# Gate one-hots of a hybrid attention, retention and expert layer: eight tokens at a time in bf16

## The chip, the cores and the metric

The kernel runs on one core of one Trainium2 chip. The metric is device time in microseconds (us), the time from the start to the end of one execution on the chip; lower is better. Five engines work side by side: TensorE (PE in the rows; PEld is its loading of weights), VectorE (DVE), ScalarE (ACT), GpSimd (POOL) and SyncE (SP), which here issues the plain DMAs. Each engine takes its instructions in the order of its own queue and waits at the head of it.

## The reference

The layer takes 1024 tokens of width 1024 in front of which 16 learned tokens are put. It adds to them the gated sum of a latent attention and a retention branch, then drops the 16 tokens and adds an expert mixer. Only the mixer matters here. Each token picks, for each of 8 heads, 16 of 128 x 128 experts, so 128 experts in all, each with a gate, and sums them:

```python
s1 = jnp.einsum('thd,kd->thk', q[..., :half], keys_1); s2 = ...   # 128 scores each
v1, i1 = lax.top_k(s1, 16); v2, i2 = lax.top_k(s2, 16)
sc, ci = lax.top_k((v1[..., :, None] + v2[..., None, :]).reshape(T, 8, 256), 16)
# e1, e2: the two key numbers (0 to 127) of each pick
eidx = e1 * 128 + e2; gates = softmax(sc)
act = gelu(einsum('td,tkd->tk', xt, peer_u[eidx]))
y = einsum('tk,tkd->td', gates * act, peer_v[eidx])
```

Inputs and outputs are float32.

## The kernel before

The 8 blocks of 128 tokens are treated in two ways. Three blocks fetch the rows of their experts by indirect DMAs that GpSimd issues (`gathered`: 256 rows of 128x1024 per block, each multiplied or accumulated on VectorE; tiles `row`, `acc`). The other five blocks, 640 tokens, are computed densely in `dense`, over all 16384 experts, and that is where the change lies.

`dense` has two halves. The first runs over `AHEAD` = 48 expert groups, called pieces here: piece `e` holds the 128 experts whose second key is `e`. For each piece, `scores(e)` loads 512 KB (`raw`), splits it into two parts that TensorE multiplies exactly (`whi` on ScalarE, line 218; `wlo` on VectorE, line 219), multiplies them with two segments of the five blocks' activations (`xT`, 384 columns wide, and `x`, 256 wide; lines 246 to 248, into tiles `tr`), applies Gelu (`gl`, line 1159) and stores the result (`gl_d`). The second half runs over groups of eight pieces: it takes `gl` from memory or computes it, multiplies it with the gates (`gt`, line 1210), and multiplies the result (`c_hi`, `c_lo`) with `peer_vt` into accumulators. It needs the gates of all 640 tokens as a dense matrix of first key by second key by token, which lies in memory as `gate_d`.

That matrix is made in `gate_matrix`, in the first half of `dense`, as background work. For each token there are two one-hot matrices of 128 picks by 128 keys: `oa` (line 1119) says which first key each pick has, `ob` (line 1120) which second key, times the pick's gate. One matmul per token (line 1105) with the picks as the contracted dimension gives that token's 128x128 gates. `kt` holds the key numbers and `gT` the gates of a block, with picks on partitions and tokens along the free dimension. Eight tokens make a step, called a batch here: 16 VectorE instructions, 8 matmuls of the batch before, one ScalarE copy out of PSUM (`stage`, line 1106); after four batches `stage` is stored to `gate_d`. There are 80 batches.

The order of background work is set by credit. After each `split_piece`, `pace` adds 6.5 (`pacing["piece"]`, 1.3 times 5 blocks) times the rate to two queues; the gates' queue has rate 0.8, the gathered rows' queue 0.45 (`RATES[4]`). A generator in a queue is advanced while its credit is above zero, and each advance takes off what it yields: 2.0 for a batch, 1.2 for a gathered row. So one piece brings 5.2 / 2.0 = 2.6 batches and 2.9 / 1.2 = 2.4 rows. After piece 47 `finish(0)` runs whatever batches are left, one after the other, and brings no rows meanwhile. Within that program order a scheduler still moves instructions of one engine's queue a little.

Of the kernel before, what the change touches and what calls it, by code (L numbers as in the profile page):

```python
# [12 lines left out]
F32 = mybir.dt.float32  # L13
BF16 = mybir.dt.bfloat16
# [3 lines left out]
AF = mybir.ActivationFunctionType  # L18
OP = mybir.AluOpType
# [4 lines left out]
P = 128  # L24
# [119 lines left out]
def hybrid_layer(ctx: ExitStack, tc: tile.TileContext, out, a, dbg=None):  # L144
    nc = tc.nc
    V, S, T, G = nc.vector, nc.scalar, nc.tensor, nc.gpsimd
    dbg = dbg or {}

    const = ctx.enter_context(tc.tile_pool(name="const", bufs=1))
# [36 lines left out]
    def load_const(name, ap, shape):  # L186
        t = const.tile(shape, F32, name=name)
        nc.sync.dma_start(t, ap)
        return t

    def bcast(ap, n, off=0):
        return bass.AP(tensor=ap.tensor, offset=ap.offset + off, ap=[[0, P], [1, n]])
# [86 lines left out]
    def zacc(name="zacc"):  # L279
        return ps.tile([P, 2, 512], F32, name=name, tag="zacc", bufs=3)  # L280
# [35 lines left out]
    def group(g):  # L316
# [530 lines left out]
        def output():  # L847
# [84 lines left out]
            def route_pairs(i):  # L932
                found = yield from choose(blocks[i], *top[i], fc, ktp)
                if ktp:
                    routed.append(found)
                else:
                    background[1].append(gathered(blocks[i], *found))
# [35 lines left out]
    def top16(tv, ti, src):  # L973
        n = src.shape[-1]
        V.max(tv[:, 0:8], src)
        V.max_index(ti[:, 0:8], tv[:, 0:8], src)
        w = work.tile([P, 128], F32, name="topw", bufs=3)
        V.match_replace(w[:, :n], tv[:, 0:8], src, NEG)
        V.max(tv[:, 8:16], w[:, :n])
        V.max_index(ti[:, 8:16], tv[:, 8:16], w[:, :n])  # L980


    def choose(b, tv, ti, fp, ktp=None):

        v1, v2 = tv[:, :, 0], tv[:, :, 1]
        cand = fp.tile([P, H, NCAND], F32, name="cand")
        V.tensor_tensor(cand[:, :, 0:16], v1[:, :, 0:1].to_broadcast([P, H, 16]), v2, OP.add)
        V.tensor_tensor(cand[:, :, 16:72].rearrange("p h (i j) -> p h i j", j=8),
                        v1[:, :, 1:8].unsqueeze(3).to_broadcast([P, H, 7, 8]),
                        v2[:, :, 0:8].unsqueeze(2).to_broadcast([P, H, 7, 8]), OP.add)  # L990
        V.tensor_tensor(cand[:, :, 72:80], v1[:, :, 8:16], v2[:, :, 0:1].to_broadcast([P, H, 8]), OP.add)
        sv = fp.tile([P, H, 16], F32, name="sv")
        si = fp.tile([P, H, 16], U32, name="si")
        yield 1.5
        for h in range(H):
            top16(sv[:, h], si[:, h], cand[:, h])
            yield 0.8

        sx = fp.tile([P, H, 16], F32, name="sx")
        V.tensor_tensor(sx, sv, sv[:, :, 0:1].to_broadcast([P, H, 16]), OP.subtract)  # L1000
        S.activation(sx, sx, AF.Exp)
        sm = work.tile([P, H], F32, name="sm")
        V.tensor_reduce(sm, sx, AX.X, OP.add)
        V.reciprocal(sm, sm)
        gate = fp.tile([P, 128], F32, name="gate") if ktp else work.tile([P, 128], F32, name="gate", bufs=NGATH)
        V.tensor_tensor(gate.rearrange("p (h k) -> p h k", h=H), sx, sm.unsqueeze(2).to_broadcast([P, H, 16]), OP.mult)


        sh = fp.tile([P, 128], I32, name="sh")
        pf = fp.tile([P, 128], F32, name="pf")  # L1010
        w1 = fp.tile([P, 128], F32, name="w1")
        w2 = fp.tile([P, 128], F32, name="w2")
        rc = fp.tile([P, 16, 2, H], BF16, name="rc")
        rcv = rc.rearrange("p k s h -> p s h k")
        sif = si.rearrange("p h k -> p (h k)")
        V.tensor_scalar(sh, sif.bitcast(I32), 3, None, op0=OP.logical_shift_right)
        V.tensor_copy(pf, sif)
        V.tensor_scalar(w1, sh, -1.0, 0.0, op0=OP.add, op1=OP.max)
        V.scalar_tensor_tensor(w1, pf, -64.0, w1, op0=OP.add, op1=OP.max)
        V.tensor_copy(rcv[:, 0], w1.rearrange("p (h k) -> p h k", h=H))  # L1020
        V.tensor_scalar(w2, w1, 8.0, 8.0, op0=OP.mult, op1=OP.add)
        V.scalar_tensor_tensor(w2, w1, 64.0, w2, op0=OP.add, op1=OP.min)
        V.scalar_tensor_tensor(w2, w1, 0.0, w2, op0=OP.is_gt, op1=OP.mult)
        V.tensor_tensor(rcv[:, 1], pf.rearrange("p (h k) -> p h k", h=H), w2.rearrange("p (h k) -> p h k", h=H),
                        OP.subtract)

        yield 3.0


        ib = fp.tile([P, 16, 2 * H], BF16, name="ib")  # L1030
        V.tensor_copy(ib.rearrange("p i (s h) -> p h s i", s=2), ti)
        e12 = fp.tile([P, 2, 128], F32, name="e12")
        ev = e12.rearrange("p s (h k) -> p k s h", h=H)
        rf = rc.rearrange("p k s h -> p k (s h)")
        for k0 in range(0, 16, 8):
            oh = fp.tile([P, 8, 16, 2 * H], BF16, name="oh")
            V.tensor_tensor(oh, rf[:, k0:k0 + 8].unsqueeze(2).to_broadcast([P, 8, 16, 2 * H]),
                            iota_i.unsqueeze(1).to_broadcast([P, 8, 16, 2 * H]), OP.is_equal)
            V.tensor_tensor(oh, oh, ib.unsqueeze(1).to_broadcast([P, 8, 16, 2 * H]), OP.mult)
            for n in (8, 4, 2):  # L1040
                V.tensor_tensor(oh[:, :, 0:n], oh[:, :, 0:n], oh[:, :, n:2 * n], OP.add)
            V.tensor_tensor(ev[:, k0:k0 + 8], oh[:, :, 0].rearrange("p k (s h) -> p k s h", s=2),
                            oh[:, :, 1].rearrange("p k (s h) -> p k s h", s=2), OP.add)
            yield 3.7
        if not ktp:
            eidx = work.tile([P, 128], I32, name="eidx", bufs=NGATH)
            V.scalar_tensor_tensor(eidx, e12[:, 0], 128.0, e12[:, 1], op0=OP.mult, op1=OP.add)
            return eidx, gate
        pt = zacc()[:, 0]
        for s in range(2):  # L1050
            T.transpose(pt[:, P * s:P * s + P], e12[:, s], ident)
        T.transpose(pt[:, 2 * P:3 * P], gate, ident)
        kt = ktp.tile([P, 2, P], F32, name=f"kt{b}")
        S.activation(kt.rearrange("p a b -> p (a b)"), pt[:, 0:2 * P], AF.Copy)
        gT = ktp.tile([P, P], F32, name=f"gT{b}")
        S.activation(gT, pt[:, 2 * P:3 * P], AF.Copy)
        return kt, gT
# [36 lines left out]
    def gate_matrix(i, kt, gT, p):  # L1094

        stage = {}

        def products(t8, pairs):
            t0 = t8 // TS * TS
            if t8 == t0:  # L1100
                stage[0] = p.tile([P, P, TS], F32, name="stage", bufs=2)
            pg = zacc()
            for q, (oa, ob) in enumerate(pairs):
                for t in range(4):
                    T.matmul(pg[:, q, P * t:P * t + P], oa[:, t], ob[:, t], start=True, stop=True)
            S.activation(stage[0][:, :, t8 - t0:t8 - t0 + 8].rearrange("p e (q t) -> p e q t", q=2),
                         pg.rearrange("p q (t e) -> p e q t", t=4), AF.Copy)
            if t8 == t0 + TS - 8:
                nc.sync.dma_start(gate_d[(P * i + t0) // TS], stage[0].rearrange("p e t -> p (e t)"))

        pending = None
        for t8 in range(0, P, 8):
            pairs = []
            for q in range(2):
                oa = p.tile([P, 4, P], F32, name="oa", bufs=4)
                ob = p.tile([P, 4, P], F32, name="ob", bufs=4)
                for t in range(4):
                    k = t8 + 4 * q + t
                    V.tensor_scalar(oa[:, t], iota, kt[:, 0, k:k + 1], None, op0=OP.is_equal)  # L1119
                    V.tensor_scalar(ob[:, t], iota, kt[:, 1, k:k + 1], gT[:, k:k + 1], op0=OP.is_equal, op1=OP.mult)  # L1120
                pairs.append((oa, ob))
            if pending:
                products(*pending)
            pending = (t8, pairs)
            yield 2.0
        products(*pending)

    def dense(xT):
# [137 lines left out]
    iota = load_const("iota", a["c_iota"], [P, P])  # L1266
    iota_i = const.tile([P, 16, 2 * H], BF16, name="iota_i")
    V.tensor_copy(iota_i, iota[:, 0:16].unsqueeze(2).to_broadcast([P, 16, 2 * H]))
    gqr = load_const("gqr", bcast(a["g_qk"], 32, 64), [P, 32])
    gkr = load_const("gkr", bcast(a["g_qk"], 32, 96 + 64), [P, 32])  # L1270
    gqk = const.tile([P, 2], F32, name="gqk")
# [44 lines left out]
```

## Time and profile before

| | us |
|---|---|
| median of three runs | 3613.85 (3611.62 to 3617.17) |
| profiled execution | 3618.72 |
| its span, first to last instruction | 3616.9 |
| TensorE busy in the span | 3343.7 |
| VectorE busy | 2788.3 |
| ScalarE busy | 1191.6 |
| GpSimd busy | 1088.5 |

The profiled execution is 4.9 us longer than the median. Busy times are sums over the whole program, whose stages have different limits. A busy TensorE record includes the time that a matmul is in the pipeline, so consecutive records overlap.

### The profile page before, as it was taken

Reading aid. Unit: us, or ns where it says so; the run is one execution under the profiler, and the core shown is the slowest. Engines: PE = TensorE matmul, PEld = TensorE weight load, DVE = VectorE, ACT = ScalarE, POOL = GpSimd, SP = SyncE. Lnnn points to the kernel's source line nnn. Section 1 sums busy time; section 2 is a strip of 40 time slices with the busy share of each in tenths; the row PEclk is TensorE's granted clock in tenths of the full one; section 3 lists DMA queues with packets and bytes.
Section 4 is the critical chain, followed back from the end, with each engine's and each line's share of the span. In section 5 each row is a group of like instructions: output and inputs, shape, how many; then the busy total and the mean of one; then the engine's idle time right before and its main releaser. Section 6 shows DMA issues by size and latency. Waiting matters only on the chain.

```text
span 3616.9 us, 54537 instructions
## 1 busy us (share of the span) xinstructions
PE 3343.7 (92%) x20376; PEld 3023.5 (84%) x20376; DVE 2788.3 (77%) x6698; ACT 1191.6 (33%) x2017; POOL 1088.5 (30%) x772
## 2 busy tenths in 40 slices
PE   8999989998799998999898899999999989999999
PEld 7888988788677898998888687888788878887788
DVE  5645569997896666899999887787778777877776
ACT  3445334544355533233333222222222222222221
POOL 0000000112011121113333355454545544544454
PEclk9999999999899998999999999999999999999999
DMA  3322454467644376455666788898889888988886
GB/s 128 119 81 98 136 189 136 150 211 242 209 145 154 123 261 242 160 174 218 267 252 259 273 313 315 286 321 293 303 281 315 279 288 297 323 298 287 287 298 247
DMA packets 329257, 837.18 MB, mean 231 GB/s; under 512 B 45712, under 2 KB 140688, under 8 KB 326176
## 3 DMA queue, kind: packets, MB, share of 16 engines
q1 hardware_dynamic: 218400, 431.00, 35.4%
q0 software_dynamic: 110592, 402.70, 31.5%
q8 instruction: 160, 2.62, 0.3%
q14 instruction: 105, 0.86, 0.1%
HBM read 755.16 MB, written 78.43 MB: 230 GB/s over the span
## 4 chain that ended last, share of the span: by engine, by line
PE 42%; DVE 20%; issue 16%; DMA 11%; POOL 8%; ACT 3%; POOLq 0%; SPq 0%; DVEq 0%; ACTq 0%
PE zacc L246 9%; PE zacc L248 9%; PE zacc L247 9%; POOL row L1065 8%; DMA row<-in_peer_v_dram,eidx 7%; DVE ob L1120 4%; DVE oa L1119 3%; DVE wlo L219 3%; DVE acc L1087 3%; PE tr L246 3%; PE tr L247 2%; PE tr L248 2%; PE tr L765 2%; DMA gt<-gate_d 2%; PE sc L729 1%
## 5 line engine op out<-in xcount | busy, mean ns | idle before, releaser
L1065 POOL DMA_INDIRECT row<-in_peer_u_dram,eidx x384 | 494.6, 1288 | 1726.3 <-DVE row L1082 837.0
L218 ACT ACTIVATE whi<-raw 128x1024 fp32r<-128x1024 f32 (+2 forms) x508 | 520.7, 1026 | 1263.4 <-PE zacc L248 626.9
L219 DVE TENSOR_TENSOR wlo<-raw,whi 128x1024 fp32r<-128x1024 f32 (+2 forms) x508 | 599.3, 1180 | 328.4 <-ACT whi L218 327.3
L1065 POOL DMA_INDIRECT row<-in_peer_v_dram,eidx x384 | 593.7, 1546 | 772.9 <-DVE acc L1087 643.9
L246 PE MATMUL zacc<-whi,c_hi 128*128 128x512 f32 x1280 | 511.2, 399 | 75.3 <-ACT c_hi L218 59.2
L1087 DVE SCALAR_TENSOR_TENSOR acc<-row,dots,acc 128x1024 f32<-128x1024 f32 x384 | 481.7, 1279 | 92.9 <-DMA row<-in_peer_v_dram,eidx 92.2
L248 PE MATMUL zacc<-whi,c_lo 128*128 128x512 f32 x1280 | 509.1, 398 | 2.0 <-DVE c_lo L219 2.0
L247 PE MATMUL zacc<-wlo,c_hi 128*128 128x512 f32 x1280 | 507.9, 397 | 0.0
L1082 DVE SCALAR_TENSOR_TENSOR row<-row,xn 128x1024 f32<-128x1024 f32 x384 | 463.7, 1219 | 55.3 <-DMA row<-in_peer_u_dram,eidx 54.5
L246 PE MATMUL tr<-xT_hi,whi 128*128 128x384 f32 (+1 forms) x1216 | 417.0, 343 | 17.9 <-ACT gl L1159 16.8
L248 PE MATMUL tr<-xT_hi,wlo 128*128 128x384 f32 (+1 forms) x1216 | 413.9, 340 | 0.0
L247 PE MATMUL tr<-xT_lo,whi 128*128 128x384 f32 (+1 forms) x1216 | 411.8, 339 | 0.0
L246 PEld LDWEIGHTS zacc<-whi,c_hi 128*128 128x128 f32 x1280 | 246.9, 193 | 132.9 <-ACT c_hi L218 62.5
L248 PE MATMUL tr<-x_hi,wlo 128*128 128x256 f32 x1024 | 300.4, 293 | 37.3 <-DVE wlo L219 37.3
L246 PE MATMUL tr<-x_hi,whi 128*128 128x256 f32 x1024 | 299.5, 292 | 11.1 <-ACT whi L218 9.1
L247 PE MATMUL tr<-x_lo,whi 128*128 128x256 f32 x1024 | 297.0, 290 | 0.0
L248 PEld LDWEIGHTS zacc<-whi,c_lo 128*128 128x128 f32 x1280 | 245.7, 192 | 60.0 <-DVE c_lo L219 8.3
L247 PEld LDWEIGHTS zacc<-wlo,c_hi 128*128 128x128 f32 x1280 | 246.7, 193 | 51.3
L246 PE MATMUL zacc<-whi,hn_hi 128*128 128x256 f32 x832 | 251.5, 302 | 3.8 <-DVE vr L679 1.3
L246 PEld LDWEIGHTS tr<-xT_hi,whi 128*128 128x128 f32 x1216 | 232.4, 191 | 20.4 <-ACT gl L1159 18.0
L247 PE MATMUL zacc<-wlo,hn_hi 128*128 128x256 f32 x832 | 239.7, 288 | 1.4 <-DVE wlo L219 1.4
L248 PE MATMUL zacc<-whi,hn_lo 128*128 128x256 f32 x832 | 238.6, 287 | 0.0
(284 smaller groups left out, 6935.6 us busy)
## 6 DMA issues: line engine op xcount, KB each, us to landing
raw<-in_peer_ut_dram SPq DMA_DIRECT2D x128, 512.0 KB, 4.8
raw<-in_peer_vt_dram SPq DMA_DIRECT2D x128, 512.0 KB, 6.6
gate_d<-stage SPq DMA_DIRECT2D x20, 2048.0 KB, 7.4
gt<-gate_d SPq DMA_DIRECT2D x32, 1280.0 KB, 14.6
raw<-in_w_nat_dram SPq DMA_DIRECT2D x72, 512.0 KB, 3.5
raw<-in_w_z_dram SPq DMA_DIRECT2D x48, 512.0 KB, 3.3
gl_d<-gl SPq DMA_DIRECT2D x48, 320.0 KB, 2.2
gl<-gl_d SPq DMA_DIRECT2D x48, 320.0 KB, 6.3
```

What stands on the lines that cost most here:

```text
L218: S.activation(hi, src, AF.Copy)
L219: V.tensor_tensor(lo, src, hi.bitcast(F32), OP.subtract)
L246: T.matmul(o, st[0], mv[0], start=first, stop=False)
L247: T.matmul(o, st[0], mv[1], start=False, stop=False)
L248: T.matmul(o, st[1], mv[0], start=False, stop=last)
L729: T.matmul(sc[:, c, 0:w], qh, kT[0:96, k0:k0 + w], start=True, stop=c < nch - 1)
L765: T.matmul(oo, vh[:, c + k], pT[:, k], start=False, stop=c + k == b)
L1065: G.indirect_dma_start(out=row, out_offset=None, in_=table, in_offset=bass.IndirectOffsetOnAxis(ap=eidx[:, k:k + 1], axis=0))
L1082: op = V.scalar_tensor_tensor(row, row, 1.0, xn, op0=OP.mult, op1=OP.mult, accum_out=dots[:, k:k + 1])
L1087: op = V.scalar_tensor_tensor(acc[k % 2], row, dots[:, k:k + 1], acc[k % 2], op0=OP.mult, op1=OP.add)
L1119: V.tensor_scalar(oa[:, t], iota, kt[:, 0, k:k + 1], None, op0=OP.is_equal)
L1120: V.tensor_scalar(ob[:, t], iota, kt[:, 1, k:k + 1], gT[:, k:k + 1], op0=OP.is_equal, op1=OP.mult)
```

## The change

The one-hots of a batch are made by four instructions in place of 16. A constant `iota_2` holds 0, 0, 1, 1, ... 127, 127 in bf16, and `kt` is kept in bf16 (integers to 127). One VectorE equality makes all eight tokens' one-hots of first keys as a bf16 tile of 4 x 128 x 2, with two tokens innermost (`eq`, n = 0, line 1117 of the changed file), a second those of second keys. ScalarE converts the first to float32 (`oa`, line 1119), VectorE multiplies the second with the gates into float32 (`ob`, line 1120). The matmuls read every second element of `oa` and `ob`. A batch now yields 1.7.

```diff
-        kt = ktp.tile([P, 2, P], F32, name=f"kt{b}")
+        kt = ktp.tile([P, 2, P], BF16, name=f"kt{b}")
...
-            for q, (oa, ob) in enumerate(pairs):
-                for t in range(4):
-                    T.matmul(pg[:, q, P * t:P * t + P], oa[:, t], ob[:, t], start=True, stop=True)
+            oa, ob = pairs
+            for t in range(8):
+                T.matmul(pg[:, t // 4, P * (t % 4):P * (t % 4) + P], oa[:, t // 2, :, t % 2], ob[:, t // 2, :, t % 2],
+                         start=True, stop=True)
...
-            pairs = []
-            for q in range(2):
-                oa = p.tile([P, 4, P], F32, name="oa", bufs=4)
-                ob = p.tile([P, 4, P], F32, name="ob", bufs=4)
-                for t in range(4):
-                    k = t8 + 4 * q + t
-                    V.tensor_scalar(oa[:, t], iota, kt[:, 0, k:k + 1], None, op0=OP.is_equal)
-                    V.tensor_scalar(ob[:, t], iota, kt[:, 1, k:k + 1], gT[:, k:k + 1], op0=OP.is_equal, op1=OP.mult)
-                pairs.append((oa, ob))
+            at = lambda t: t.rearrange("p (q r) -> p q r", r=2).unsqueeze(2).to_broadcast([P, 4, P, 2])
+            eq = [p.tile([P, 4, P, 2], BF16, name=f"eq{n}", bufs=2) for n in range(2)]
+            for n in range(2):
+                V.tensor_tensor(eq[n], iota_2.unsqueeze(1).to_broadcast([P, 4, P, 2]), at(kt[:, n, t8:t8 + 8]), OP.is_equal)
+            pairs = [p.tile([P, 4, P, 2], F32, name=n, bufs=2) for n in ("oa", "ob")]
+            S.activation(pairs[0], eq[0], AF.Copy)
+            V.tensor_tensor(pairs[1], eq[1], at(gT[:, t8:t8 + 8]), OP.mult)
...
-            yield 2.0
+            yield 1.7
...
+    iota_2 = const.tile([P, P, 2], BF16, name="iota_2")
+    V.tensor_copy(iota_2, iota.unsqueeze(2).to_broadcast([P, P, 2]))
```

The change moves instructions in three queues. In VectorE's queue, in the middle of the gates, the kernel before has after each `wlo` 16 short `oa` and `ob` instructions for each batch, of which the first four stand here:

```order
L1087 SCALAR_TENSOR_TENSOR acc_7090<-row,dots,acc_7090 128x1024
L219 TENSOR_TENSOR wlo<-raw,whi 128x1024
L1119 TENSOR_SCALAR oa<-iota,kt_12501 128x128
L1120 TENSOR_SCALAR ob<-iota,kt_12501,gT_12503 128x128
L1119 TENSOR_SCALAR oa<-iota,kt_12501 128x128
L1120 TENSOR_SCALAR ob<-iota,kt_12501,gT_12503 128x128
```

In the changed kernel the same queue has, from the rows of one piece to those of the next (`eq` is either equality):

```order
L1087 SCALAR_TENSOR_TENSOR acc_7093<-row,dots,acc_7093 128x1024
L1117 TENSOR_TENSOR eq_18888<-iota_138,kt_12503 128x1024
L1120 TENSOR_TENSOR ob<-eq_18889,gT_12505 128x1024
L1117 TENSOR_TENSOR eq_18907<-iota_138,kt_12503 128x1024
L1117 TENSOR_TENSOR eq_18908<-iota_138,kt_12503 128x1024
L1117 TENSOR_TENSOR eq_18925<-iota_138,kt_12503 128x1024
L1117 TENSOR_TENSOR eq_18926<-iota_138,kt_12503 128x1024
L219 TENSOR_TENSOR wlo<-raw,whi 128x1024
L1120 TENSOR_TENSOR ob<-eq_18908,gT_12505 128x1024
L1117 TENSOR_TENSOR eq_19021<-iota_138,kt_17036 128x1024
L1120 TENSOR_TENSOR ob<-eq_18926,gT_12505 128x1024
L1087 SCALAR_TENSOR_TENSOR acc_7092<-row,dots,acc_7092 128x1024
```

The piece's `wlo` now stands amid its three batches, behind equalities of the last of them, and about 9 gate instructions a piece (3.06 batches of 3) take the place of 42 (2.6 batches of 16). In TensorE's queue of the kernel before, the gate matmuls of a batch are spread one by one between a piece's products:

```order
L1105 MATMUL zacc<-ob,oa 128x128
L248 MATMUL tr<-x_hi_15494,wlo 128x256
L246 MATMUL tr<-x_hi_15494,whi 128x256
L1105 MATMUL zacc<-ob,oa 128x128
L247 MATMUL tr<-x_lo_15495,whi 128x256
```

In the changed kernel a batch's eight, or two batches' 16, stand together, with the first products of the next piece between them:

```order
L248 MATMUL tr<-xT_hi,wlo 128x384
L1105 MATMUL zacc<-ob,oa 128x128 x16
L246 MATMUL tr<-x_hi_15496,whi 128x256
L247 MATMUL tr<-x_lo_15497,whi 128x256
L248 MATMUL tr<-x_hi_15496,wlo 128x256
L1105 MATMUL zacc<-ob,oa 128x128 x8
```

The first product that reads `wlo` (line 248) now comes right behind the 16. In SyncE's queue, at the end of the first half, the kernel before stores the last gates behind the last result of a piece (`gl_d`), then loads the running sums (`y`) and the first gates (`gt`):

```order
L1186 DMA gl_d<-gl 128x640
L1109 DMA gate_d<-stage 128x4096 x2
L1151 DMA raw<-in_peer_ut_dram 128x1024
L1109 DMA gate_d<-stage 128x4096
L1233 DMA raw<-in_peer_vt_dram 128x1024 x2
```

In the changed kernel two pieces' results and their loads follow the last gates:

```order
L1110 DMA gate_d<-stage 128x4096
L1185 DMA gl_d<-gl 128x640
L1150 DMA raw<-in_peer_ut_dram 128x1024
L1110 DMA gate_d<-stage 128x4096
L1185 DMA gl_d<-gl 128x640
L1232 DMA raw<-in_peer_vt_dram 128x1024
L1194 DMA y_21053<-h_d 128x1024
```

One more `gl_d` follows three rows further down. The gates end ahead of the results of the last two pieces, where before they ended behind them.

## Rows read from the trace of the kernel before

**Rows 1.** The page's busy times over the span, and instruction counts.
```profile
PE 3343.7 (92%) x20376; PEld 3023.5 (84%) x20376; DVE 2788.3 (77%) x6698; ACT 1191.6 (33%) x2017; POOL 1088.5 (30%) x772
```

**Rows 2.** Busy time by stretch: gates amid pieces, gates alone, turn, second half.
```profile
core 0: us, PE busy (x) PEld busy (x) DVE busy (x) ACT busy (x) POOL busy (x), PEclk, DMA share, GB/s
1633.70:2005.90 372.20, 337.33 (x2456) 327.25 (x2455) 370.04 (x1245) 122.31 (x156) 125.60 (x67) 0.98 0.66 250
2005.90:2038.60 32.70, 29.59 (x137) 19.77 (x135) 32.70 (x133) 8.78 (x9) 5.12 (x3) 1.00 0.48 187
2038.60:2082.00 43.40, 27.98 (x188) 27.46 (x188) 25.56 (x22) 6.19 (x11) 22.80 (x15) 0.90 0.96 356
2082.00:3616.90 1534.90, 1446.80 (x7488) 1276.36 (x7488) 1181.11 (x1427) 358.75 (x486) 769.79 (x543) 0.97 0.85 296
```

**Rows 3.** Groups by line, 1633.7 to 2038.8 us: busy us, mean ns | idle before.
```profile
L1120 DVE TENSOR_SCALAR ob<-iota,kt,gT 128x128 f32<-128x128 f32 x640 | 216.7, 339 | 0.0
L1119 DVE TENSOR_SCALAR oa<-iota,kt 128x128 f32<-128x128 f32 x640 | 182.2, 285 | 0.0
L1087 DVE SCALAR_TENSOR_TENSOR acc<-row,dots,acc 128x1024 f32<-128x1024 f32 x71 | 87.3, 1274 | 2.2 <-DMA row<-in_peer_v_dram,eidx 2.2
L246 PE MATMUL tr<-xT_hi,whi 128*128 128x384 f32 x220 | 77.2, 351 | 0.0
L246 PE MATMUL tr<-x_hi,whi 128*128 128x256 f32 x217 | 69.6, 321 | 0.0
L219 DVE TENSOR_TENSOR wlo<-raw,whi 128x1024 fp32r<-128x1024 f32 x26 | 31.5, 1213 | 0.0
```

**Rows 4.** Waits, 1633.7 to 2038.8 us: total us, times, longest.
```profile
POOL row L1065 <- DVE acc L1087: 245.4, 30, 11.5
ACT stage L1106 <- PE zacc L1105: 205.1, 71, 7.6
PE tr L248 <- DVE wlo L219: 35.5, 22, 4.2
```

**Rows 5.** Timeline of TensorE at 1761 us: start, length, one batch's 16 records.
```profile
1761.34 1.95 PE L1105 MATMUL zacc<-ob,oa 128*128 128x128 f32 x16
```

**Rows 6.** Timeline of SyncE at 1530 us: two pieces without gates, back to back.
```profile
1530.72 0.33 SPq L1186 DMA_DIRECT2D gl_d<-gl  x1
...
1537.70 0.33 SPq L1186 DMA_DIRECT2D gl_d<-gl  x1
```

**Rows 7.** Timeline of ScalarE, 2019 to 2039 us: two of six copies, gates alone.
```profile
2027.20 1.02 ACT L1106 ACTIVATE stage<-zacc 128x1024 f32<-128x1024 f32 x1 [2.64 <-PE zacc L1105]
2030.77 1.02 ACT L1106 ACTIVATE stage<-zacc 128x1024 f32<-128x1024 f32 x1 [2.54 <-PE zacc L1105]
```

**Rows 8.** Timeline of SyncE, 2000 to 2100 us: last piece, last gates, first load.
```profile
2005.91 0.32 SPq L1186 DMA_DIRECT2D gl_d<-gl  x1
...
2039.07 0.34 SPq L1109 DMA_DIRECT2D gate_d<-stage  x1
...
2057.57 0.46 SPq L1209 DMA_DIRECT2D gt<-gate_d  x1
```

**Rows 9.** Waits, 2038 to 2100 us: TensorE at the turn.
```profile
PE zacc L246 <- ACT c_hi L218: 14.1, 1, 14.1
```

**Rows 10.** Groups by line and shape, whole span: VectorE's nearest operations.
```profile
L219 DVE TENSOR_TENSOR wlo<-raw,whi 128x1024 fp32r<-128x1024 f32 x469 | 572.4, 1221 | 311.6 <-ACT whi L218 310.6 <-issue 0.3
L1041 DVE TENSOR_TENSOR oh<-oh 128x1024 bf16<-128x1024 bf16 x16 | 10.9, 680 | 0.0
L1037 DVE TENSOR_TENSOR oh<-rc,iota_i 128x2048 bf16<-128x2048 bf16 x16 | 19.5, 1217 | 0.0
L1006 DVE TENSOR_TENSOR gate<-sx,sm 128x128 f32<-128x128 f32 x8 | 2.7, 335 | 0.0
L1022 DVE SCALAR_TENSOR_TENSOR w<-w,w 128x128 f32<-128x128 f32 x8 | 2.3, 284 | 0.0
```

**Rows 11.** Groups by line and shape, whole span: ScalarE's nearest operation.
```profile
L218 ACT ACTIVATE whi<-raw 128x1024 fp32r<-128x1024 f32 x469 | 496.2, 1058 | 1211.3 <-PE zacc L248 622.7 <-PE tr L247 361.3 <-PE zacc L247 148.0
```

## The prediction

> **What bounds the kernel now.** I read the page's busy times first: TensorE is busy for 3343.7 of 3616.9 us, so over the whole program it looks like the bound [rows 1]. A stage can have another bound, so I cut the span around the gates, from the first `oa` at 1633.7 us to the end of the last at 2038 us, into stretches [rows 2]. There VectorE is busy for 370.04 of 372.20 us while gates and pieces run side by side, and for 32.70 of 32.70 us while the gates left over run alone. It has no gap at all: this stage is VectorE's.
>
> Who works there is in the groups by line [rows 3]. Busy times of the short `oa` and `ob` overlap, so I take the gates' share as the rest: 402.7 us of VectorE, less 71 row accumulations (87 us) and 26 `wlo` (31.5 us), is 284 us, or 3.55 us for each of 80 batches. The stretch with gates alone confirms it: ScalarE's copies of finished batches start 3.57 us apart [rows 7].
>
> What does TensorE need in the same stage? A batch's 16 matmul records take 1.95 us [rows 5]. A piece without gates takes 6.98 us, the distance of two results with nothing between [rows 6]. The first product of a piece's eight is there 220 and 217 times [rows 3], so 27.3 pieces. That makes 80 x 1.95 + 27.3 x 6.98 = 156 + 191 = 347 us, where the stage takes 405 us (372.2 + 32.7). TensorE has 58 us of slack, and its largest wait there is for `wlo`, 35.5 us, the queue of VectorE again [rows 4]. ScalarE waits 205.1 us for gate matmuls and GpSimd 245.4 us for accumulations [rows 4]; neither is near a bound.
>
> Two things follow the stage. 32.7 us of it come after the last piece's result at 2005.9 us [rows 8]: some nine batches that the credit had not brought out (2.6 per piece, so 71 in 27.3 pieces). And at the turn to the second half TensorE waits 14.1 us [rows 9], because the first `gt` is issued only at 2057.57 us [rows 8] and lands when the pieces at hand are used up.
>
> **The change part by part.**
>
> *Equalities.* 128x1024 in bf16, two per batch. The nearest row is the bf16 `oh` addition of that size, 680 ns [rows 10]; the float32 operation of that size takes 1221 ns [rows 10]. Whether the bf16 price holds when one operand is a pair read 128 times over, no row shows. Ends: 680 and 1221 ns. I take 0.68 us, since element count, types and output are those of the row.
>
> *Scaling.* Bf16 times float32 into float32, 128x1024: no cheaper than the float32 row, 1.22 us [rows 10]. A batch costs VectorE 2 x 0.68 + 1.22 = 2.58 us in place of 3.55, with the other end at 3.66. For 80 batches that is 206 us. With the unchanged 87 and 31.5 us VectorE needs 325 us. That is below TensorE's 347, so the bound passes to TensorE.
>
> *Conversion on ScalarE.* The nearest row is 1.06 us for 128x1024 [rows 11], so 80 x 1.06 = 85 us more. ScalarE was busy for 131 of 405 us [rows 2]; 216 of about 370 leaves cover. Without cover it would cost 1.06 us per batch.
>
> *Matmul operands with every second element.* No row has such an operand. I take nothing. The moving side has room: a piece streams 24 x 384 + 24 x 256 = 15360 columns in 6.98 us [rows 6], 2.2 per ns, a batch 2048 in 1.95 us [rows 5], 1.05 per ns. The loading of weights shows no such room, so the other end is a doubling, 3.9 us a batch.
>
> *Yield 1.7.* 5.2 / 1.7 = 3.06 batches per piece, so 80 batches are out after 26.2 pieces and none is left for `finish(0)`. The gates alone with TensorE half idle go away; the remaining 1.1 pieces run without gates. Accumulations per piece stay 2.4, so the second half begins with the same rows done.
>
> *New waits.* A piece's TensorE queue is now 16 gate matmuls, two products, the first product that needs `wlo`, and 8 more gate matmuls. VectorE's queue has `ob`, an equality and `wlo` in a row. The tiles `oa` and `ob` hold two batches, so that `ob` waits for the first half of the 16. From there VectorE needs 1.22 + 0.68 + 1.21 = 3.1 us to `wlo`, and TensorE arrives after 1.95 us (the other half) and 0.24 us (two products). It waits 0.9 us per piece, 24 us for 26.2 pieces. Queued behind that product are 45 products and 8 gate matmuls, and the `stage` copies wait for those. Ends: nothing, if VectorE is let in earlier, and 2 us per piece, if ScalarE's conversion is late as well.
>
> *The turn.* The last gates come before the results of two pieces, whose 14 us of products lie over the store and the load of the first `gt`. I give back 9 of the 14.1 us; ends 0 and 14. The `iota_2` constant is one operation at the start, under 1 us.
>
> *Sum.* Stage: 347 + 24 = 371 in place of 405 us, 34 saved; turn 9 saved; 43 us. The profiled execution is 3618.7 us, so 3575.7, and it lies 4.9 us above the median of the runs shown: **3571 us**. With the waits at nothing and the turn closed, 58 + 14 = 72 us would be saved: 3542 us.
>
> **Rules weighed against it.** The L1006 row reads one word of `sm` 16 times in a row and takes 335 ns, where an operation of that size without it takes 284 [rows 10], 0.4 ns more per word. An equality reads 512 such words: 0.68 + 0.2 = 0.88 us. [...] By the row a batch is 2 x 0.88 + 1.22 = 2.98 us, VectorE needs 357 us, the wait per piece grows to 1.1 us, and the stage takes about 376 to 380: 3576 to 3580 us, still my case. [...]
>
> **The rivals.**
>
> *The equalities run at the float32 price.* Batch 3.66 us, VectorE 293 + 118 = 411 us; it stays the bound and the stage as long as before. Only the turn gains, 9 less 6: about 3611 us. For it: no row has pairs as innermost run. Against it: the `oh` equality on line 1037, where `rc` is read 16 times over in runs of 16, runs at 1217 / 2048 = 0.6 ns per element, half the float32 price [rows 10].
>
> *A chain of queues eats more.* Each batch now passes VectorE, ScalarE, TensorE and ScalarE again, and ScalarE's queue has the copies of finished batches, which wait for TensorE (205.1 us of such waits already [rows 4]), ahead of the next conversion. At 2 us per piece the stage takes 347 + 52 = 399: about 3599 us. Against it: 3.1 us of work per batch on ScalarE in 4.2 us of time is far from full.
>
> *Slower: the step in the weights.* If TensorE loads every second word at half the rate, a batch costs 3.9 us, the stage 191 + 312 + 24 = 527 us, 122 more, less 9 at the turn: 3727 us. It decides once a batch costs over (405 + 9 - 24 - 191) / 80 = 2.49 us, 28% more than now. For it: 16 loads in 1.95 us stand one behind the other without room. Against it: the words read are whole float32 words, and only their distance changes.
>
> *The saving is given back in the second half.* Its DMA engines are 85% busy [rows 2]. If the gathered rows held that half up, it would lengthen by what the stage gained; TensorE is busy for 1446.8 of its 1534.9 us [rows 2], and the number of rows left is the same, so little speaks for it: about 3612 us.
>
> **How the numbers follow.** Chances: my case 0.55 (3542 to 3588), the chain of queues 0.17 (3588 to 3608), float32 price 0.10 (3606 to 3612), the step in the weights 0.12 (3625 to 3727), given back 0.06 (3608 to 3616). The range 3540 to 3612 leaves out the slower rival and a part of the last, under 0.2. A measurement of this kernel can tell about 0.2%, 7 us. Faster by more than that, below 3606.6: 0.55 + 0.17 and a part of the float32 case, 0.77. Slower, above 3621: 0.11. Within: 0.12.
>
> **What would show it.** Equalities of 0.68 us (0.88 by the repeated word, 1.22 by the rival), `ob` of 1.22, `oa` of 1.05 on ScalarE; VectorE with gaps in the stage and TensorE without, apart from about a microsecond before line 248 for each piece; 16 gate records still in 1.95 us; no stretch of gates without pieces; the last gates some 45 to 60 us earlier; a wait at the turn below 14 us; a second half of 1535 us. A stage of over 400 us, or 16 records in over 2.4 us, would make the forecast wrong, and the rows say which.

## The result, and the profile after

The changed kernel takes 3566.07 us (median of 4 runs, 3562.51 to 3571.28), the kernel before on the same chip 3612.98 us. The ratio is 0.9869, 95% interval 0.9852 to 0.9886: 47 us faster. On two further chips, beside the experiments, its ratio was 0.9854 (0.9832 to 0.9876) and 0.9881 (0.9865 to 0.9896). The profiled execution has a span of 3569.5 us, against 3616.9. The forecast of 3571 us was close; several of its terms were not, as the rows show.

The page's busy times of the changed kernel:

```profile
PE 3322.8 (93%) x20376; PEld 3022.3 (85%) x20376; DVE 2687.7 (75%) x5659; ACT 1268.1 (36%) x2097; POOL 1090.4 (31%) x772
```

Against [rows 1] VectorE lost 101 us and 1039 instructions, ScalarE gained 77 us and 80 instructions, TensorE has the same number of records. Busy times by stretch of the changed kernel: from the first equality to a piece's end behind the last gates, the turn, the second half; then the whole way from the first equality to the first product with `c_hi`:

```profile
core 0: us, PE busy (x) PEld busy (x) DVE busy (x) ACT busy (x) POOL busy (x), PEclk, DMA share, GB/s
1632.80:1980.70 347.90, 340.76 (x2551) 339.76 (x2550) 303.23 (x336) 205.33 (x242) 159.09 (x70) 0.99 0.76 284
1980.70:2041.00 60.30, 40.24 (x249) 39.25 (x249) 33.36 (x31) 11.73 (x19) 21.41 (x16) 0.83 0.84 300
2041.00:3569.50 1528.50, 1441.14 (x7470) 1271.84 (x7468) 1172.28 (x1418) 354.90 (x479) 745.73 (x542) 0.97 0.85 296
...
1632.80:2036.63 403.83, 376.63 (x2779) 375.42 (x2778) 332.96 (x363) 214.89 (x258) 177.66 (x85) 0.97 0.77 287
```

In the first stretch TensorE is busy for 340.76 of 347.90 us and VectorE for 303.23: the bound has passed from one to the other. The last row is the fairest measure of what was gained, because it ends at an event that both kernels have, the first product that reads `c_hi`. In the kernel before it starts half a microsecond behind the cut of [rows 2]:

```profile
2082.50 0.79 PE L246 MATMUL zacc<-whi,c_hi 128*128 128x512 f32 x1 [14.09 <-ACT c_hi L218]
```

Up to it the kernel before ran 2082.50 - 1633.70 = 448.8 us, with 2456 + 137 + 188 = 2781 TensorE records [rows 2], the changed kernel 403.83 us with 2779. That is 45.0 us for the same work. From there to the end it is 3616.9 - 2082.5 = 1534.4 us before and 3569.5 - 2036.63 = 1532.9 us after: the second half gave nothing back. A difference of this size says no more than that, because two profiled executions of one and the same kernel (yield 2.0, below) differ there by 10 us (1523.0 and 1532.8).

The costliest groups, 1600 to 2030 us (busy us, mean ns, idle before, as in [rows 3]):

```profile
L1087 DVE SCALAR_TENSOR_TENSOR acc<-row,dots,acc 128x1024 f32<-128x1024 f32 x87 | 108.1, 1279 | 27.5 <-DMA row<-in_peer_v_dram,eidx 27.5
L1117 DVE TENSOR_TENSOR eq<-iota,kt 128x1024 bf16<-128x1024 bf16 x160 | 102.8, 683 | 0.6
L1120 DVE TENSOR_TENSOR ob<-eq,gT 128x1024 f32<-128x1024 bf16 x80 | 97.3, 1217 | 1.2 <-PE zacc L1105 1.2
L1119 ACT ACTIVATE oa<-eq 128x1024 f32<-128x1024 bf16 x80 | 84.3, 1053 | 29.1 <-DVE eq L1117 29.1
L219 DVE TENSOR_TENSOR wlo<-raw,whi 128x1024 fp32r<-128x1024 f32 x35 | 42.7, 1221 | 29.6 <-ACT whi L218 29.6
```

An equality takes 683 ns, where the plain bf16 addition of that size took 680 [rows 10], so the pair that it reads 128 times over has no price. A batch costs VectorE 2 x 0.683 + 1.217 = 2.58 us where it was 3.55. VectorE now waits ahead of `wlo`, for ScalarE's `whi` (29.6 us), and ahead of the accumulations, for the rows' transfers (27.5 us). Apart from one place, told below, it is early and not late.

The timeline of TensorE, two batches with the second element's step (start, length, records), and of SyncE, two results of pieces in the middle of the gates:

```profile
1760.11 3.92 PE L1105 MATMUL zacc<-ob,oa 128*128 128x128 f32 x32
```

```profile
1799.93 0.32 SPq L1185 DMA_DIRECT2D gl_d<-gl  x1
1812.71 0.32 SPq L1185 DMA_DIRECT2D gl_d<-gl  x1
```

32 records in 3.92 us are 1.96 us a batch, where it was 1.95 [rows 5]. Pieces come 12.78 us apart. A piece alone takes 6.98 us [rows 6], and 6.98 + 3 x 1.95 = 12.83: a piece and its three batches stand end to end on TensorE, with no wait in them.

The waits of TensorE (total us, times, longest), first from 1632.8 to 1990 us, then from 1990 to 2060 us:

```profile
PE zacc L1105 <- ACT gl L1158: 6.2, 1, 6.2
PE zacc L1105 <- DVE ob L1120: 1.0, 1, 1.0
...
PE tr L246 <- ACT gl L1158: 20.1, 1, 20.1
PE zacc L246 <- ACT c_hi L218: 7.6, 1, 7.6
```

The 35.5 us for `wlo` [rows 4] are gone. The wait of 6.2 us is new. It comes early in the gates, and VectorE's queue says why (VectorE's timeline, then TensorE's):

```profile
1692.18 1.28 DVE L1087 SCALAR_TENSOR_TENSOR acc<-row,dots,acc 128x1024 f32<-128x1024 f32 x1 [7.06 <-DMA row<-in_peer_v_dram,eidx]
1696.55 1.83 PE L1105 MATMUL zacc<-ob,oa 128*128 128x128 f32 x7 [6.16 <-ACT gl L1158]
```

An accumulation waits 7.06 us for its row, and the next equalities stand behind it in VectorE's queue; ScalarE's `oa`, which waits 9.33 us for its equality, and a Gelu stand behind those.

At the turn there were 14.1 us of wait [rows 9], all ahead of the first product with `c_hi`. Now there are 20.1 us ahead of it and 7.6 us behind it, 27.7 in all. The 20.1 us are for a Gelu, which itself takes ScalarE 0.47 us (2022.81 below). ScalarE's timeline says why:

```profile
1996.35 0.39 ACT L1158 ACTIVATE gl<-tr 128x256 f32<-128x256 f32 x1 [1.63 <-issue]
2022.17 0.74 ACT L218 ACTIVATE c_hi<-gl 128x640 fp32r<-128x640 f32 x1 [25.44 <-DVE gl L1209]
2022.81 0.47 ACT L1158 ACTIVATE gl<-tr 128x384 f32<-128x384 f32 x1
```

The first `c_hi` stands in ScalarE's queue ahead of a piece's Gelu (line 1158) and waits 25.44 us there for VectorE's product with the gates (line 1209). VectorE's wait (1990 to 2060 us) and SyncE's timeline carry the chain further back:

```profile
DVE gl L1209 <- DMA gt<-gate_d: 17.1, 2, 9.1
```

```profile
1990.14 1.75 SPq L1194 DMA_DIRECT2D y<-h_d  x3
...
1993.43 0.91 SPq L1194 DMA_DIRECT2D y<-h_d  x2
1994.39 0.42 SPq L1208 DMA_DIRECT2D gt<-gate_d  x1
```

`gt` was issued at 1994.39 us, 63 us sooner than before [rows 8], but behind five loads of `y` of 512 KB. While its product waits, TensorE has a result of line 246 to 248 in PSUM that nobody reads, and about 13 us of pieces that it can't begin (2023.34, the end of the wait, to 2036.63).

The first group of the second half has two such `gt`. The second is issued at 2039.73 us, VectorE's product waits 8.0 us for it, and TensorE's wait of 7.6 us follows from that:

```profile
2057.99 0.79 PE L246 MATMUL zacc<-whi,c_hi 128*128 128x512 f32 x1 [7.56 <-ACT c_hi L218]
```

This wait cost a little more than its length. From 2023.34 to 2028.00 us, behind the 20.1 us, TensorE's granted clock is 0.53, and from 2028 to 2032 us it is 1.00. The products with `xT` start 0.32 us apart from 2023.82 to 2027.66 us, and 0.17 us apart behind 2028.05 us. The kernel before shows 0.50 from 2082 to 2086 us, behind its own wait.

### The profile page after: what moved, and what is told of

It reads as the page before. It is cut to its first block, busy times and chain, and to the rows that moved or that the text cites. A ratio compares the mean times of both kernels' runs of the same rounds, so it can differ in the third digit from the quotient of the medians.

```text
span 3569.5 us, 53608 instructions
## 1 busy us (share of the span) xinstructions
PE 3322.8 (93%) x20376; PEld 3022.3 (85%) x20376; DVE 2687.7 (75%) x5659; ACT 1268.1 (36%) x2097; POOL 1090.4 (31%) x772
## 4 chain that ended last, share of the span: by engine, by line
PE 49%; issue 17%; DMA 13%; DVE 11%; POOL 6%; ACT 3%; POOLq 0%; SPq 0%; DVEq 0%; ACTq 0%
PE zacc L246 10%; PE zacc L248 10%; PE zacc L247 10%; DMA row<-in_peer_v_dram,eidx 7%; POOL row L1065 6%; PE tr L246 4%; PE tr L247 4%; PE tr L248 4%; DMA gt<-gate_d 3%; DVE wlo L219 2%; PE tr L765 2%; PE sc L729 1%; DVE acc L1087 1%; ACT whi L218 1%; DMA row<-in_peer_u_dram,eidx 1%
## 5 line engine op out<-in xcount | busy, mean ns | idle before, releaser
L1065 POOL DMA_INDIRECT row<-in_peer_u_dram,eidx x384 | 486.3, 1266 | 1731.5 <-DVE row L1082 839.9
L1065 POOL DMA_INDIRECT row<-in_peer_v_dram,eidx x384 | 603.9, 1573 | 718.5 <-DVE acc L1087 605.4
L248 PE MATMUL tr<-x_hi,wlo 128*128 128x256 f32 x1024 | 290.1, 283 | 0.0
```

The lines of the kernel that those rows point to most:

```text
L248: T.matmul(o, st[1], mv[0], start=False, stop=last)
L1065: G.indirect_dma_start(out=row, out_offset=None, in_=table, in_offset=bass.IndirectOffsetOnAxis(ap=eidx[:, k:k + 1], axis=0))
```

## The experiments

The theory after the result: the one-hots' 16-bit price and ScalarE's conversion free VectorE; the yield of 1.7 doesn't help, and what it does at the turn costs. Rivals: the gain is in the yield, or in few long instructions instead of many short ones, or in the turn. Times are medians, ratios are to the kernel before on the same chip.

**The yield alone.** The kernel before with

```diff
-            yield 2.0
+            yield 1.7
```

> The kernel before with one change: a batch of gates yields 1.7 in place of 2.0. Theory (VectorE's cheaper one-hots are the gain): VectorE's need is still 284 + 87 + 32 = 403 us for gates, accumulations and wlo, so the stage stays VectorE's and stays as long; the batches alone at its end go, which moves work but saves VectorE nothing; 3600 to 3615 us. Rival (the earlier end of the gates is the gain): most of the 47 us come already here, 3565 to 3580 us.

Measured: 3627.84 us, ratio 1.0039 (1.0024 to 1.0053): slower by 0.4%, and above the 3600 to 3615 us that the theory gave. Waits of TensorE, 1633 to 1980, then 1980 to 2110 us:

```profile
PE tr L248 <- DVE wlo L219: 29.8, 17, 4.2
...
PE tr L248 <- DVE wlo L219: 9.8, 5, 4.1
PE tr L246 <- ACT gl L1159: 6.7, 1, 6.7
PE zacc L246 <- ACT c_hi L218: 6.1, 1, 6.1
```

VectorE is the bound as before (it sits idle for 2.9 us in all ahead of its 640 `oa`), so the waits for `wlo` stay, and gates brought forward gain nothing: the first product with `c_hi` starts at 2084.00 us, 1.5 us later than in the kernel before. The profiled execution is 9.4 us longer (3626.3 against 3616.9), so most of the loss lies behind that product. The wait of 6.1 us for `c_hi` is there, at 2103.86 us, where the kernel before has none; the changed kernel has its 7.6 us at the same place. The wait for a Gelu, too, comes with the yield. The yield is no source of the gain.

**The one-hots alone.** The changed kernel with

```diff
-            yield 1.7
+            yield 2.0
```

> The changed kernel with the yield of 2.0 put back. Theory: 71 batches beside 27.3 pieces, 71 x 1.95 + 27.3 x 6.98 = 329 us of TensorE, then nine alone at VectorE's 2.6 us each, 23 us: 352 us in place of 355, so 3560 to 3575 us, nearly all of the gain; what differs is the turn to the second half. Rival (the yield is needed): batches alone at the end cost as before, 3585 us or more.

Measured: 3553.61 us, ratio 0.9838 (0.9813 to 0.9863): below the 3560 to 3575 us of its theory, and below the whole change (0.9869), though the intervals overlap here; the yields are timed on one chip below. TensorE's timeline at the turn, the busy times up to there, and ScalarE's timeline:

```profile
2022.25 0.79 PE L246 MATMUL zacc<-whi,c_hi 128*128 128x512 f32 x1 [17.19 <-ACT c_hi L218]
```

```profile
1632.80:2022.25 389.45, 372.26 (x2781) 371.24 (x2779) 330.28 (x360) 214.12 (x257) 179.12 (x86) 0.98 0.82 300
```

```profile
1998.88 0.47 ACT L1158 ACTIVATE gl<-tr 128x384 f32<-128x384 f32 x1
...
2021.46 2.16 ACT L218 ACTIVATE c_hi<-gl 128x640 fp32r<-128x640 f32 x3 [15.48 <-DVE gl L1209]
```

The same 2781 records are done in 389.45 us, 14 us less than with 1.7. The first `c_hi` is ready at the same time in both (2021.46 us here, 2022.17 us in the changed kernel). The difference is what TensorE had left to do then: here all pieces were finished and only 17.2 us were idle; there 13 us of pieces were still to come, shut in behind `c_hi`. ScalarE's queue agrees: here one more Gelu (1998.88) stands ahead of the first `c_hi`, and three `c_hi` follow together. The wait for a second `gt`, 7.6 us in the changed kernel, is not there either.

**The conversion on VectorE.** The changed kernel with

```diff
-            S.activation(pairs[0], eq[0], AF.Copy)
+            V.tensor_copy(pairs[0], eq[0])
```

> The changed kernel with the conversion of the first operand moved from ScalarE to VectorE. Theory: TensorE bounds the stage with 12.8 us per piece, and VectorE needs 3.06 x 2.58 + 2.4 x 1.2 + 1.2 = 12.0 us, so it has under 1 us per piece to spare; a conversion costs 0.6 to 1.2 us, three of them per piece make VectorE the bound again with 13.9 to 15.7 us: 26 pieces, 20 to 65 us longer than the changed kernel, 3586 to 3631 us. Rival (VectorE has room, since the wait for wlo that I forecast is not there): within 5 us of the changed kernel's 3566.

Measured: 3593.22 us (2 runs), ratio 0.9935 (0.9914 to 0.9956). The group of the conversion, 1600 to 2050 us, and TensorE's wait for `wlo`, 1633 to 1990 us:

```profile
L1119 DVE CAST oa<-eq 128x1024 f32<-128x1024 bf16 x80 | 54.9, 686 | 0.1
```

```profile
PE tr L248 <- DVE wlo L219: 13.0, 7, 3.5
```

A batch is now 3.27 us on VectorE, which is busy for 346.73 of 361.20 us (1632.8 to 1994 us), and the last gate product starts at 1992.8 us instead of 1972.4. Half of the gain is lost (0.9935 against 0.9869), as expected. The place on ScalarE matters, and ScalarE had the room: with the conversions there it is busy for 205.33 of 347.90 us in the changed kernel. The trace shows a part of the way: the first product with `c_hi` starts 10.6 us later than in the changed kernel (2047.25 against 2036.63), where the whole profiled execution is 22.2 us longer (3591.7 against 3569.5); the rest lies in the second half, and no run shows why.

**Equalities in float32.** The changed kernel with

```diff
-        kt = ktp.tile([P, 2, P], BF16, name=f"kt{b}")
+        kt = ktp.tile([P, 2, P], F32, name=f"kt{b}")
...
-            eq = [p.tile([P, 4, P, 2], BF16, name=f"eq{n}", bufs=2) for n in range(2)]
+            eq = [p.tile([P, 4, P, 2], F32, name=f"eq{n}", bufs=2) for n in range(2)]
...
-    iota_2 = const.tile([P, P, 2], BF16, name="iota_2")
+    iota_2 = const.tile([P, P, 2], F32, name="iota_2")
```

> The changed kernel with key numbers, constant and equalities in float32 in place of bf16, the rest the same (as few instructions, pairs innermost, conversion on ScalarE now a copy). Theory (the price of 16-bit operands is the gain): 1.22 us an equality, 3.66 a batch, VectorE 15.4 us per piece, stage about 411 us as before the change: 3615 to 3630 us. Rival (few long instructions in place of many short ones are the gain): an equality well under 1.2 us, and 3566 to 3590 us.

Measured: 3639.87 us, ratio 1.0066 (1.0051 to 1.0082), above the 3615 to 3630 us of its theory. The equalities' group, 1600 to 2060 us, and TensorE's waits, 1633 to 2010 us:

```profile
L1117 DVE TENSOR_TENSOR eq<-iota,kt 128x1024 f32<-128x1024 f32 x160 | 188.1, 1216 | 0.0
```

```profile
PE zacc L1105 <- DVE ob L1120: 43.8, 25, 9.2
```

Four long instructions in place of 16 short ones gain nothing by themselves: 3 x 1.22 = 3.65 us for a batch, against 3.55. The 16-bit price is the gain. Beside the first experiment, which has the yield of 1.7 with the short instructions, this run is 12.0 us slower (3639.87 against 3627.84); the dearer batch makes 80 x 0.1 = 8 us of that as an estimate, and the rest was not tried apart.

**The gates' load ahead of the sums' loads.** The changed kernel with `gt` issued before `y` (the five `y` loads move behind the first `weights` of the second half):

```diff
-        ys = []
         for b in range(NGATH, NBLK):
-            ys.append(vp.tile([P, D], F32, name=f"y{b}"))
-            nc.sync.dma_start(ys[-1], h2_d[b])
...
+        ys = [vp.tile([P, D], F32, name=f"y{b}") for b in range(NGATH, NBLK)]
...
+            if not e0:
+                for y, b in zip(ys, range(NGATH, NBLK)):
+                    nc.sync.dma_start(y, h2_d[b])
```

> The changed kernel with the second half's first gt load issued ahead of the y loads on SyncE's queue; nothing else moved. Theory (the wait of 20.1 us at the turn is gt's transfer queued behind 2.6 MB of y, with the conversion that needs it standing ahead of a piece's Gelu on ScalarE): the wait of VectorE's product for gt ends 8 to 12 us sooner, TensorE's wait for the Gelu shrinks by as much, first product with c_hi about 2026, time 3554 to 3560 us. Rival (the second half gives the turn's time back, or the wait has another end): 3563 to 3569 us, as the changed kernel.

The same with a yield of 2.0:

> The same gt order with a yield of 2.0 us, so that the four pieces asked for ahead are done before the wait. Theory: the yield of 2.0 took 12 us off the changed kernel and left 17.2 us of wait at the turn; with gt ahead of y, 8 to 12 us of that go: 3541 to 3548 us. Rival (nothing but the yield counts): 3551 to 3556 us, as the run with the yield of 2.0 alone.

The first again, with `finish(0)` and the first `gt` placed ahead of the last piece instead of behind it:

> The gt order of the run before, a yield of 1.7, and the weights' finish with the gate load placed one piece earlier in the program, so that ScalarE's queue has one more piece's Gelu ahead of the first c_hi. Theory: the Gelu that TensorE waited for is no longer behind c_hi: wait at the turn under 8 us, 3546 to 3556 us. Rival (order on ScalarE doesn't matter, only gt's arrival): as the run with gt first alone. Rival (turn is given back): 3563 to 3569 us.

And the changed kernel beside them:

> The changed kernel itself on the same chip, for the comparison: 3563 to 3569 us, ratio 0.985 to 0.989 on every theory.

Measured, on one chip:

| | us | ratio to before (95%) | first product with `c_hi` |
|---|---|---|---|
| changed kernel | 3569.59 | 0.9854 (0.9832 to 0.9876) | 2032.35 |
| `gt` first | 3567.05 | 0.9853 (0.9829 to 0.9877) | 2027.28 |
| `gt` first, `finish(0)` a piece earlier | 3563.54 | 0.9844 (0.9819 to 0.9868) | 2025.57 |
| `gt` first, yield 2.0 | 3556.18 | 0.9834 (0.9810 to 0.9858) | 2013.12 |

The mechanism was right at its place. From the issue of `gt` to the first `c_hi` it takes 2022.17 - 1994.39 = 27.8 us in the changed kernel and 25.1 us with the yield of 2.0, but with `gt` first this (SyncE's timeline, then ScalarE's):

```profile
1989.61 0.49 SPq L1205 DMA_DIRECT2D gt<-gate_d  x1
```

```profile
2004.66 0.74 ACT L218 ACTIVATE c_hi<-gl 128x640 fp32r<-128x640 f32 x1 [8.88 <-DVE gl L1206]
```

It is 2004.66 - 1989.61 = 15.1 us: 10 to 13 us of the longer times had been the queue of `y`. TensorE's waits at the turn (1985 to 2110 us):

```profile
PE tr L246 <- ACT gl L1158: 7.1, 2, 4.2
PE zacc L246 <- ACT c_hi L218: 5.4, 1, 5.4
```

Yet the time didn't follow as expected: all three missed their ranges, and none differs from its twin without the new order by more than the intervals. With the yield of 2.0 the trace shows where it went. The first product comes 9 us sooner than without the new order (2013.12 against 2022.25), but in the 50 us from it TensorE does 149 records and is busy for 37.85 us, against 209 records in 50.00 us (first with `gt` first, then without):

```profile
2013.12:2063.12 50.00, 37.85 (x149) 29.89 (x149) 33.27 (x34) 9.28 (x11) 21.05 (x15) 0.90 0.85 295
```

```profile
2022.25:2072.25 50.00, 50.00 (x209) 41.10 (x210) 41.83 (x43) 12.21 (x15) 22.77 (x16) 0.94 0.87 299
```

Its waits with `gt` first, from 1985 to 2110 us:

```profile
PE zacc L246 <- ACT c_hi L218: 7.5, 1, 7.5
PE tr L246 <- ACT gl L1158: 6.2, 1, 6.2
PE zacc L246 <- DVE y L1242: 4.5, 1, 4.5
```

The waits for `c_hi` and `y`, 12.0 us, now lie behind the first product: the second `gt` and the running sums come late instead of the first `gt`. With the yield of 1.7 the first product is 5 us sooner than in the changed kernel beside it; whether these 5 us reach the end is open, since the medians differ by 2.5 us and single runs by up to 16. To place `finish(0)` a piece earlier changed neither the wait (8.0 us for the Gelu) nor, by more than the interval, the time. It was meant to bring one more Gelu ahead of the first `c_hi`, but ScalarE's timelines of the two runs show `c_hi` behind the same Gelu (1995.31 us with `gt` first, 1995.73 us here), so the order on ScalarE was not tried by this run, and no other moves it alone.

**The yield again, on one chip.** The changed one-hots with three yields:

> The changed one-hots with the yield of 2.0 kept, timed beside the changed kernel on one chip. Theory (the yield of 2.0 spreads the gates over more of the first half, so that no piece is left whose Gelu can stand behind the first c_hi): 10 to 14 us below the changed kernel, 3552 to 3557 us. Rival (the earlier difference of 12 us was one of chips): within 4 us of the changed kernel.

> The changed one-hots with a yield of 2.3, 2.26 batches for each piece, so that some 11 batches are left for the end of the first half. Theory: the batches left over run alone, bound by VectorE at 2.58 us or more each, about 28 us with no piece beside them, while some 12 pieces ran without all their gates: 3565 to 3580 us, above the yield of 2.0. Rival (the fewer gates amid pieces the better): below 3550 us.

> The changed kernel on the same chip, for the comparison of yields: 3563 to 3570 us.

| yield | us | ratio to before (95%) | waits of TensorE at the turn |
|---|---|---|---|
| 1.7 | 3571.39 | 0.9881 (0.9865 to 0.9896) | Gelu 15.7, `c_hi` 7.1 |
| 2.0 | 3554.75 | 0.9831 (0.9818 to 0.9844) | `c_hi` 17.2 |
| 2.3 | 3572.42 | 0.9884 (0.9869 to 0.9899) | `c_hi` 28.3, `y` 4.9 |

The difference of 17 us between 1.7 and 2.0 stands, with intervals apart and above the 10 to 14 us of its theory, so it was not one of chips. With the 6.2 us in the gates, which of the three only the yield of 1.7 has, the waits add up to 29.0 us with 1.7 and 17.2 us with 2.0; the two profiled executions are 9.8 us apart (3568.1 and 3558.3). With 2.3 the last gates are stored later, SyncE issues `gt` at 2009.71 us in place of 1998.80, and the wait grows by as much. The time of that run is in its range, but what lengthens it is this wait; its theory had spoken of the batches left over. TensorE's timeline with 2.3:

```profile
2035.50 0.80 PE L246 MATMUL zacc<-whi,c_hi 128*128 128x512 f32 x1 [28.27 <-ACT c_hi L218]
```

The changed one-hots with the yield of 2.0 are the best version found, 60 us below the kernel before and 17 us below the changed kernel; `gt` first added nothing to them (0.9834).

## Why the prediction was right, and where only in its sum

**The bound of the stage** was VectorE, and it passed to TensorE, as forecast: 340.76 busy of 347.90 us. Bring the float32 price back and the gain is gone (ratio 1.0066); bring the conversion back to VectorE and half of it is (0.9935).

**Equalities at 0.68, scaling at 1.22, conversion at 1.06 us:** 683, 1217 and 1053 ns. The dearer price by the repeated word, 0.88 us, drawn from line 1006 of [rows 10], did not come: one pair to a run is as cheap here as the operands of the plain bf16 addition (680 ns), and what made line 1006 dearer stays open.

**The step in the weights at nothing:** right, 1.96 us a batch, and a load of weights for these matmuls takes 198 ns, 192 before.

**The wait for `wlo`, 24 us, was the first mis-sized term: it is nil.** The step held `ob` back until half of a batch's matmuls had read its tile. The row of `ob` shows 1.2 us of such waits in all 80 batches. VectorE's queue ran ahead by more than that and even waited 29.6 us for `whi`. What the prediction kept as the lower end ("nothing, if VectorE is let in earlier") is what happened. Up to the first product with `c_hi` 45.0 us were gained, although TensorE has 6.2 us of new wait in the gates and 20.1 us at the turn in place of 14.1. Without these it would have been 45.0 + 6.2 + 6.0 = 57.2 us: the slack of 58 us that the prediction had read between TensorE's need and the stage.

**The turn, 9 us to be saved, was the second: it cost 6.0 us ahead of the first product with `c_hi`, and 7.6 us behind it.** The prediction saw that two pieces would lie over the load of `gt`, and took for granted that TensorE could work on them. It looked at SyncE's and TensorE's queues, but not at ScalarE's, where the first `c_hi` stands ahead of a Gelu that those pieces need. In other profiled executions of the changed kernel the wait for the Gelu was 14.5 and 15.7 us, so its size varies, but not its place. The 6.2 us in the gates are a third term, which the prediction had only as a rival: a chain of queues, here from a row's transfer to a Gelu.

That the sum came out is luck. Up to the first product, 24 us for a wait that was not there stand against 9 + 6.0 us at the turn and 6.2 us in the gates that were missed; they cancel to 3 us.

**Yield 1.7**, which the prediction counted as a gain by closing the stretch of gates alone, is a loss of 17 us against 2.0. The left-over batches that it avoids are cheap now: with 2.0 those at the end start 2.49 us apart (1970.37, 1972.85 and 1975.34 us on TensorE's timeline), where they took 3.57 [rows 7]. And pieces that are done ahead of the wait were worth more here than gates done early.

**The second half** stayed as it was, 1532.9 us for 1534.4, as forecast, though it has the 7.6 us of wait now; what made up for them was not traced, and they are within what that half differs by from one execution to the next.

## What to carry to other kernels

When work of a stage is brought forward, look for what stands behind the next stage's first wait in every queue, also of engines that are mostly idle: here, as the traces have it, one conversion on an engine that is 36% busy shut in 13 us of TensorE's work. A pacing constant that was tuned with one bound should be measured again by itself after the bound has moved; here 0.3 of it (1.7 against 2.0) was worth 17 us, a third of the change. One-hot equalities in 16 bits, several tokens to an instruction with the tokens innermost, were to be had here at 683 ns against 1216 in float32, and the step that they left in the matmul operands was free here (1.96 us for a batch's 16 records, against 1.95).

## What was not expected of the hardware

A bf16 equality whose second operand is one pair repeated 128 times ran at 683 ns for 1024 elements to a partition, the price of a plain bf16 addition of that size (680 [rows 10]). Converting bf16 to float32 took VectorE 686 ns, while multiplying bf16 by float32 into float32 took 1217: the 32-bit output alone did not bring the dearer price here. Whether the float32 operand does, or the second operand beside such an output, is not shown. ScalarE needed 1053 ns for the same conversion. Float32 matmul operands with every second element, as weights and as moving data, took 1.96 us for a batch's 16 records, against 1.95 without the step.
